# A weight gradient's block products: Strassen's seven for eight in ten of 32 pairs of slices

## The chip, the cores and the metric

The kernel runs on one core of a Trainium2 chip. The metric is the device time of one execution in microseconds; the kernel before takes 176.07 us (median of 3 runs, 175.95 to 176.48). The profiled execution spans 174.3 us from its first to its last instruction.

## The reference

```python
batch, m, k, n = 16, 512, 1024, 768      # float32 inputs, drawn from a normal distribution

def reference(input, grad_output):
    grad_weight = np.einsum('bmk,bmn->kn', input, grad_output)
    return grad_weight.astype(np.float32)
```

With batch and m joined, this is one matrix product: OUT (1024 x 768) = X^T G, with X of 8192 x 1024 and G of 8192 x 768, summed over 8192 rows. Both kernels cut the rows into 64 slices of 128 rows. A slice of X is 128 partitions by 1024 columns, a slice of G is 128 by 768. Both are turned to bf16 on their way into SBUF (the first ones by VectorE and ScalarE), are multiplied on TensorE and summed in fp32.

## The kernel before

TensorE multiplies one slice in twelve matmuls that are all 512 columns wide. The output's first 512 columns are computed as they stand: eight tiles of 128 rows of OUT (parts A and B, four tiles each), with X as the stationary operand. The last 256 columns (part N) are computed transposed: G's columns are stationary, X moves, and the result is turned back by VectorE in 32 x 32 blocks before it is stored.

```python
P = 128
NA = 512
WARMUP = [512] * 10 + [128] * 2
XBUFS = 42
...
    nc.sync.dma_start(out=gf[:, 0:NA], in_=G[0:P, 0:NA])
    nc.scalar.dma_start(out=xf[0], in_=X[0:P, :])
    nc.sync.dma_start(out=gf[:, NA:N], in_=G[0:P, NA:N])
    nc.scalar.dma_start(out=xf[1], in_=X[P : 2 * P, :])
...
    for s in range(1, S):
        gt = xg.tile([P, N], bf16, name="gt")
        nc.gpsimd.dma_start(out=gt, in_=G[s * P : (s + 1) * P, :])
        ...
        if s > 1:
            xs[s] = xg.tile([P, K], bf16, name="xt")
            nc.gpsimd.dma_start(out=xs[s], in_=X[s * P : (s + 1) * P, :])
...
    def add_out(dst, src):
        nc.vector.tensor_add(out=dst, in0=src, in1=dst)
...
    def wide_mm(bank, k, s, start, stop, c0=0, c1=NA):                       # parts A and B
        nc.tensor.matmul(
            bank, xs[s][:, k * P : (k + 1) * P], gwide[s][:, c0:c1], start=start, stop=stop
        )

    def narrow_mm(bank, t, h, s, start, stop):                               # part N
        nc.tensor.matmul(
            bank,
            gnarrow[s].rearrange("p (r t) -> p t r", t=NT)[:, t],
            xs[s][:, h * NA : (h + 1) * NA],
            start=start, stop=stop,
        )
```

A part accumulates slices in its four PSUM banks (each 128 x 512 fp32; there are eight banks) until it is closed, marked `!` in the order. Then each bank is copied (the first time) or added to a sum in SBUF, and the bank can be opened by another part:

```python
ORDER = (
    "A1! B1 N1 B2! N2 A2 N3! A3 B3 A4! B5 N5 B6! N7 A6 N8! A9! B10 N9 B12! N12! A12! "
    "B15 AB17! n17! AB26! n26! AB41! n41! AB47 A50! B50! N64!"
).split()
...
        dst = part.dst(*group)
        if part.first:
            copy_out(dst, bank, i)
            if s == 0 and i == 0:
                round_by("DVE", g0, gf, NA, N)
        else:
            add_out(dst, bank)
...
    for k in range(KS):
        slices = range(parts["A" if k < KS // 2 else "B"].done, S)
        pieces = [(0, NA)] if k < KS - 1 else [(0, 256), (256, 384), (384, NA)]
        for c0, c1 in pieces:
            ...
            for s in slices:
                wide_mm(bank, k, s, s == slices[0], s == slices[-1], c0, c1)
            add_out(acc[:, k, c0:c1], bank)
            ...
                nc.sync.dma_start(out=OUT[:, k, c : c + W], in_=acc[:, k, c : c + W])
```

"B15", for example, means: bring part B up to slice 15; "A50!" means: up to slice 50, and close. After the order the last 14 slices of A and B are done bank by bank, and every finished row tile is stored.

Of the kernel before, what the change touches and what calls it, by code (L numbers as in the profile page):

```python
# [6 lines left out]


P = 128
NA = 512  # L10
SQ = 32

ORDER = (
    "A1! B1 N1 B2! N2 A2 N3! A3 B3 A4! B5 N5 B6! N7 A6 N8! A9! B10 N9 B12! N12! A12! "
    "B15 AB17! n17! AB26! n26! AB41! n41! AB47 A50! B50! N64!"
).split()  # L20

WARMUP = [512] * 10 + [128] * 2
XBUFS = 42


@with_exitstack
def kernel(
# [6 lines left out]
    nc = tc.nc  # L34
    bf16 = mybir.dt.bfloat16
    f32 = mybir.dt.float32

    B, M, K = input.shape
    _, _, N = grad_output.shape
    S = B * M // P  # L40
    KS = K // P
    NB = N - NA
    NT = NB // P
    KH = K // NA

    X = input.rearrange("b m k -> (b m) k")
    G = grad_output.rearrange("b m n -> (b m) n")
    OUT = out.rearrange("(ks p) n -> p ks n", p=P)

    head = ctx.enter_context(tc.tile_pool(name="head", bufs=1))  # L50
    xg = ctx.enter_context(tc.tile_pool(name="xg", bufs=XBUFS))
    accp = ctx.enter_context(tc.tile_pool(name="accp", bufs=1))
    psum = ctx.enter_context(tc.tile_pool(name="psum", bufs=1, space=bass.MemoryType.PSUM))

    acc = accp.tile([P, KS, NA], f32, name="acc")
    acct = accp.tile([P, NT, K], f32, name="acct")


    turned = accp.tile([P, K // SQ, SQ, NT], f32, name="turned")


    xs = [None] * S
    gwide = [None] * S
    gnarrow = [None] * S

    E = mybir.EngineType
    ctx.enter_context(tc.manual_schedule(engines={E.PE, E.DVE, E.Activation}))


    xf = [head.tile([P, K], f32, name=f"xf{s}") for s in range(2)]  # L70
    gf = head.tile([P, N], f32, name="gf")
    nc.sync.dma_start(out=gf[:, 0:NA], in_=G[0:P, 0:NA])
    nc.scalar.dma_start(out=xf[0], in_=X[0:P, :])
    nc.sync.dma_start(out=gf[:, NA:N], in_=G[0:P, NA:N])
    nc.scalar.dma_start(out=xf[1], in_=X[P : 2 * P, :])


    ones = nc.const_aps.tensor(1.0, (P, P), bf16)
    wps = psum.tile([P, NA], f32, name="bank7")
    for i, cols in enumerate(WARMUP):  # L80
        nc.tensor.matmul(  # L81
            wps[:, 0:cols],
            ones,
            nc.const_aps.tensor(1.0, (P, cols), bf16),
            start=True,
            stop=True,
        )


    for s in range(1, S):  # L90
        gt = xg.tile([P, N], bf16, name="gt")
        nc.gpsimd.dma_start(out=gt, in_=G[s * P : (s + 1) * P, :])  # L92
        gwide[s] = gt[:, 0:NA]
        gnarrow[s] = gt[:, NA:N]
        if s > 1:
            xs[s] = xg.tile([P, K], bf16, name="xt")
            nc.gpsimd.dma_start(out=xs[s], in_=X[s * P : (s + 1) * P, :])  # L97

    for s in range(2):
        xs[s] = head.tile([P, K], bf16, name=f"x{s}")  # L100
    g0 = head.tile([P, N], bf16, name="g0")
    gwide[0] = g0[:, 0:NA]
    gnarrow[0] = g0[:, NA:N]

    def round_by(engine, dst, src, c0, c1):
        copy = nc.vector.tensor_copy if engine == "DVE" else nc.scalar.copy
        copy(out=dst[:, c0:c1], in_=src[:, c0:c1])  # L107

    round_by("DVE", g0, gf, 0, 256)
    round_by("ACT", g0, gf, 256, NA)  # L110
    round_by("DVE", xs[0], xf[0], 0, P)
    round_by("ACT", xs[0], xf[0], 2 * P, 4 * P)
    round_by("DVE", xs[0], xf[0], P, 2 * P)
    round_by("DVE", xs[0], xf[0], 4 * P, 6 * P)
    round_by("ACT", xs[0], xf[0], 6 * P, 8 * P)

    def add_out(dst, src):
        nc.vector.tensor_add(out=dst, in0=src, in1=dst)  # L118

    def copy_out(dst, src, i):  # L120
        if i % 2 == 0:
            nc.vector.tensor_copy(out=dst, in_=src)  # L122
        else:
            nc.scalar.copy(out=dst, in_=src)  # L124

    def wide_mm(bank, k, s, start, stop, c0=0, c1=NA):
        nc.tensor.matmul(  # L127
            bank, xs[s][:, k * P : (k + 1) * P], gwide[s][:, c0:c1], start=start, stop=stop
        )

    def narrow_mm(bank, t, h, s, start, stop):


        nc.tensor.matmul(  # L134
            bank,
            gnarrow[s].rearrange("p (r t) -> p t r", t=NT)[:, t],
            xs[s][:, h * NA : (h + 1) * NA],
            start=start,
            stop=stop,
        )  # L140

    class Part:
        def __init__(self, matmul, groups, dst):
            self.matmul = matmul
            self.groups = groups
            self.dst = dst
            self.done = 0
            self.first = True
            self.banks = {}

    wide_dst = lambda k: acc[:, k, :]
    narrow_dst = lambda t, h: acct[:, t, h * NA : (h + 1) * NA]
    parts = {
        "A": Part(wide_mm, [(k,) for k in range(KS // 2)], wide_dst),
        "B": Part(wide_mm, [(k,) for k in range(KS // 2, KS)], wide_dst),
        "N": Part(narrow_mm, [(t, h) for h in range(KH) for t in range(NT)], narrow_dst),
    }
    free = [f"bank{i}" for i in range(8)]

    def open_bank(part, i):  # L160
        name = free.pop(0)
        part.banks[i] = (name, psum.tile([P, NA], f32, name=name))

    def add_slice(part, i, s, first, last):
        group = part.groups[i]
        name, bank = part.banks[i]
        part.matmul(bank, *group, s, first, last)
        if not last:
            return
        dst = part.dst(*group)  # L170
        if part.first:
            copy_out(dst, bank, i)
            if s == 0 and i == 0:
                round_by("DVE", g0, gf, NA, N)
        else:
            add_out(dst, bank)
        if part is parts["N"] and s == S - 1:
            t, h = group
            hb = NA // SQ
            nc.vector.transpose(  # L180
                out=turned[:, h * hb : (h + 1) * hb, :, t],
                in_=dst.rearrange("p (b r) -> p b r", r=SQ),
            )
        free.append(name)
        del part.banks[i]
        if not part.banks:
            part.first = False

    def slice_by_slice(names, upto, close):
        while any(parts[n].done < upto for n in names):  # L190
            for n in names:
                part = parts[n]
                s = part.done
                if s == upto:
                    continue
                part.done += 1
                first = not part.banks
                for i in range(len(part.groups)):
                    if first:
                        open_bank(part, i)  # L200
                for i in range(len(part.groups)):
                    add_slice(part, i, s, first, close and s == upto - 1)

    def bank_by_bank(part, upto):
        first = part.done
        part.done = upto
        for i in range(len(part.groups)):
            open_bank(part, i)
            for s in range(first, upto):
                add_slice(part, i, s, s == first, s == upto - 1)  # L210

    for i, step in enumerate(ORDER):
        if i == 2:

            round_by("DVE", xs[1], xf[1], 4 * P, 6 * P)
            round_by("ACT", xs[1], xf[1], 6 * P, 8 * P)
            round_by("DVE", xs[1], xf[1], 0, 2 * P)
            round_by("ACT", xs[1], xf[1], 2 * P, 4 * P)
        close = step.endswith("!")
        names = step.rstrip("!").rstrip("0123456789")  # L220
        upto = int(step.rstrip("!").lstrip("ABNn"))
        if names.islower():
            bank_by_bank(parts[names.upper()], upto)
        else:
            slice_by_slice(names, upto, close)

    rows_of = out.rearrange("(b r) n -> r b n", r=SQ)
    for a in range(P // SQ):
        c = NA + a * NT * SQ
        nc.scalar.dma_start(  # L230
            out=rows_of[:, :, c : c + NT * SQ],
            in_=turned[a * SQ : (a + 1) * SQ].rearrange("p b r t -> p b (r t)"),
        )


    for k in range(KS):
        slices = range(parts["A" if k < KS // 2 else "B"].done, S)
        pieces = [(0, NA)] if k < KS - 1 else [(0, 256), (256, 384), (384, NA)]
        for c0, c1 in pieces:
            name = free.pop(0)  # L240
            bank = psum.tile([P, NA], f32, name=name)[:, 0 : c1 - c0]
            for s in slices:
                wide_mm(bank, k, s, s == slices[0], s == slices[-1], c0, c1)
            add_out(acc[:, k, c0:c1], bank)
            free.append(name)
            W = NB if k < 6 else c1 - c0
            for c in range(c0, c1, W):
                nc.sync.dma_start(out=OUT[:, k, c : c + W], in_=acc[:, k, c : c + W])


# [28 lines left out]
```

## Time and profile before

| | before |
|---|---|
| device time | 176.07 us (175.95 to 176.48) |
| span of the profiled execution | 174.3 us, 2013 instructions |
| matmuls of 512 columns, parts A and B (L127) | 489 recorded, modelled length 379 ns each |
| matmuls of 512 columns, part N (L134) | 250 recorded, 379 ns each |
| weight loads, 128 x 128 bf16 | 98 ns each |
| VectorE adding a 512-column bank to its sum | 683 ns each |
| bytes read from HBM, written to it | 58.72 MB, 3.15 MB |
| granted TensorE clock | 1.000 |

Engines are named PE (TensorE, with its weight loads as PEld), DVE (VectorE), ACT (ScalarE), POOL (GpSimd) and SP (SyncE, here an issuer of stores). L127 means line 127 of the kernel. A matmul's recorded length overlaps the next one's, so the busy time of PE says little of its pace; a few matmuls are missing from the records. In a line of groups or of the timeline, "128x512 f32<-128x512 f32" is the shape and type of output and input; what stands in brackets at its end is how long the engine stood idle just before, and what released it.

### The profile page before, as it was taken

Reading aid. Unit: us, or ns where it says so; the run is one execution under the profiler, and the core shown is the slowest. Engines: PE = TensorE matmul, PEld = TensorE weight load, DVE = VectorE, ACT = ScalarE, POOL = GpSimd, SP = SyncE. Lnnn points to the kernel's source line nnn. Section 1 sums busy time; section 2 is a strip of 40 time slices with the busy share of each in tenths; the row PEclk is TensorE's granted clock in tenths of the full one; section 3 lists DMA queues with packets and bytes.
Section 4 is the critical chain, followed back from the end, with each engine's and each line's share of the span. In section 5 each row is a group of like instructions: output and inputs, shape, how many; then the busy total and the mean of one; then the engine's idle time right before and its main releaser. Section 6 shows DMA issues by size and latency. Waiting matters only on the chain.

```text
span 174.3 us, 2013 instructions
## 1 busy us (share of the span) xinstructions
PE 169.9 (97%) x793; PEld 78.4 (45%) x808; DVE 61.3 (35%) x103; ACT 6.2 (4%) x12; POOL 66.7 (38%) x129
## 2 busy tenths in 40 slices
PE   8999999999999999999999999999999999999993
PEld 3444444444444444444444444444444444444463
DVE  0655582883940039300000662200560003931122
ACT  2640000000000000000000000000000000000000
POOL 7444434444444444444444444444274200000000
PEclk9999999999999999999999999999999999999999
DMA  5999999999999999999999999999999990085623
GB/s 192 276 208 209 207 209 208 208 208 209 207 208 209 207 208 210 207 209 209 206 209 208 208 210 207 207 209 208 207 209 209 207 202 11 0 190 160 170 86 120
DMA packets 25048, 33.35 MB, mean 191 GB/s; under 512 B 6480, under 2 KB 16592, under 8 KB 25040
## 3 DMA queue, kind: packets, MB, share of 16 engines
q0 software_dynamic: 18000, 28.65, 89.9%
q10 hardware_dynamic: 4448, 2.10, 4.7%
q1 hardware_dynamic: 2592, 2.49, 4.2%
q8 instruction: 6, 0.10, 0.2%
q14 instruction: 2, 0.02, 0.0%
HBM read 58.72 MB, written 3.15 MB: 355 GB/s over the span
## 4 chain that ended last, share of the span: by engine, by line
PE 97%; issue 0%; DVE 0%
PE bank L127 63%; PE bank L134 32%; PE bank L81 3%; DVE acc L118 0%
## 5 line engine op out<-in xcount | busy, mean ns | idle before, releaser
L127 PE MATMUL bank<-gt,xt 128*128 128x512 bf16 (+2 forms) x515 | 108.3, 367 | 0.5
L127 PEld LDWEIGHTS <-xt 128*128 128x128 bf16 x524 | 50.2, 98 | 57.2
L118 DVE TENSOR_TENSOR acc<-bank,acc 128x512 f32<-128x512 f32 (+2 forms) x62 | 37.9, 667 | 73.4 <-PE bank L127 72.9
L134 PE MATMUL bank<-xt,gt 128*128 128x512 bf16 x242 | 54.8, 379 | 0.3
L97 POOL DMA_DIRECT2D xt<-in_input_dram x62 | 33.1, 533 | 38.7 <-DMA xt<-in_input_dram 36.5
L92 POOL DMA_DIRECT2D gt<-in_grad_output_dram x63 | 33.8, 536 | 31.2 <-DMA gt<-in_grad_output_dram 24.9
L134 PEld LDWEIGHTS <-gt 128*128 128x128 bf16 x252 | 24.6, 98 | 29.7
L118 DVE TENSOR_TENSOR acct<-bank,acct 128x512 f32<-128x512 f32 x24 | 15.7, 682 | 30.0 <-PE bank L134 29.9
L81 PE MATMUL bank<-const-bfloat16-1.0 128*128 128x512 bf16 (+1 forms) x12 | 4.6, 574 | 0.8 <-PEq L263 0.8
L81 PEld LDWEIGHTS <-const-bfloat16-1.0 128*128 128x128 bf16 x12 | 1.6, 140 | 3.5 <-issue 3.5
L122 DVE COPY acc<-bank 128x512 f32<-128x512 f32 x4 | 2.7, 687 | 1.0 <-PE bank L127 1.0
L180 DVE STREAM_TRANSPOSE turned<-acct 128x512 f32<-128x512 f32 x4 | 2.9, 715 | 0.1
L127 PEld LDWEIGHTS <-x 128*128 128x128 bf16 x16 | 1.6, 98 | 1.9 <-DVE x L107 0.2
L107 DVE CAST g<-gf 128x256 bf16<-128x256 f32 x2 | 0.6, 290 | 4.7 <-DMA gf<-in_grad_output_dram 4.7
L124 ACT COPY acc<-bank 128x512 f32<-128x512 f32 x4 | 2.1, 589 | 1.3 <-PE bank L127 1.3
L127 PE MATMUL bank<-gt,x 128*128 128x512 bf16 x8 | 2.1, 379 | 0.0
L127 PE MATMUL bank<-g,x 128*128 128x512 bf16 x8 | 2.0, 398 | 0.0
L122 DVE COPY acct<-bank 128x512 f32<-128x512 f32 x2 | 1.3, 686 | 1.3 <-PE bank L134 1.3
L107 ACT CAST x<-xf 128x256 bf16<-128x256 f32 x4 | 1.4, 409 | 0.0
L107 ACT ACT_TABLE_LOAD x1 | 1.3, 1283 | 1.7 <-PEq L263 1.7
L124 ACT COPY acct<-bank 128x512 f32<-128x512 f32 x2 | 1.1, 588 | 1.5 <-PE bank L134 1.5
L107 DVE CAST x<-xf 128x256 bf16<-128x256 f32 (+1 forms) x5 | 1.0, 260 | 0.0
(8 smaller groups left out, 3.3 us busy)
## 6 DMA issues: line engine op xcount, KB each, us to landing
xt<-in_input_dram POOLq DMA_DIRECT2D x62, 256.0 KB, 8.5
gt<-in_grad_output_dram POOLq DMA_DIRECT2D x63, 192.0 KB, 8.5
out_dram<-acc SPq DMA_DIRECT2D x13, 128.0 KB, 2.7
xf<-in_input_dram ACTq DMA_DIRECT2D x2, 512.0 KB, 5.1
out_dram<-turned ACTq DMA_DIRECT2D x4, 256.0 KB, 3.4
gf<-in_grad_output_dram SPq DMA_DIRECT2D x1, 256.0 KB, 3.9
out_dram<-acc SPq DMA_DIRECT2D x1, 256.0 KB, 2.0
gf<-in_grad_output_dram SPq DMA_DIRECT2D x1, 128.0 KB, 4.7
```

Of the source, the lines that this page charges most:

```text
L81: nc.tensor.matmul(wps[:, 0:cols], ones, nc.const_aps.tensor(1.0, (P, cols), bf16), start=True, stop=True,)
L92: nc.gpsimd.dma_start(out=gt, in_=G[s * P : (s + 1) * P, :])
L97: nc.gpsimd.dma_start(out=xs[s], in_=X[s * P : (s + 1) * P, :])
L107: copy(out=dst[:, c0:c1], in_=src[:, c0:c1])
L118: nc.vector.tensor_add(out=dst, in0=src, in1=dst)
L122: nc.vector.tensor_copy(out=dst, in_=src)
L124: nc.scalar.copy(out=dst, in_=src)
L127: nc.tensor.matmul(bank, xs[s][:, k * P : (k + 1) * P], gwide[s][:, c0:c1], start=start, stop=stop)
L134: nc.tensor.matmul(bank, gnarrow[s].rearrange("p (r t) -> p t r", t=NT)[:, t], xs[s][:, h * NA : (h + 1) * NA], start=start, stop=stop,)
L180: nc.vector.transpose(out=turned[:, h * hb : (h + 1) * hb, :, t], in_=dst.rearrange("p (b r) -> p b r", r=SQ),)
```

## The change

The 64 slices are taken as 32 pairs. In 22 pairs each slice is multiplied plainly, now in sixteen matmuls of 384 columns: four parts A, B, C, D for the four quarters of OUT (upper and lower 512 rows, left and right 384 columns), each with four row tiles. Nothing is computed transposed any more.

In ten pairs the two slices (0 and 1) with the halves of X's and G's columns (left L, right R) form a 2 x 2 block product, which Strassen's scheme does with seven block products in place of eight, so 28 matmuls in place of 32. As the code forms them:

- m = (X0L + X1R)^T (G0L + G1R), n = (X0R + X1R)^T G0L, o = X0L^T (G0R - G1R), p = X1R^T (G1L - G0L), q = (X0L + X1L)^T G1R
- (X1L - X1R)^T (G1L + G1R) goes straight into part A, (X0R - X0L)^T (G0L + G0R) straight into part D
- at the end A gets m + p - q, B gets o + q, C gets n + p, and D gets m - n + o.

VectorE builds the sums and differences of X and G in bf16 (six instructions a pair) and combines the five product sums in fp32 (24 instructions at the end). A planned order says which part takes which slices when, when its four banks are closed, and how many of VectorE's extra instructions are queued before each bank's copy ("6,0,0,0") or before a step ("12A35"). Two parts of four banks are open at most. The purpose is less work for TensorE, with VectorE's free time in exchange.

The diff, cut to its core:

```diff
-NA = 512
-SQ = 32
+LOADS = "sssssssssssssssPsPPPPPPPPPssssss"
 ORDER = (
-    "A1! B1 N1 B2! N2 A2 N3! A3 B3 A4! B5 N5 B6! N7 A6 N8! A9! B10 N9 B12! N12! A12! "
-    "B15 AB17! n17! AB26! n26! AB41! n41! AB47 A50! B50! N64!"
+    "A1 C1!0,0,0,0 D1 D2!0,0,0,0 A2 B1 B2!0,0,0,0 A3 C2 C3 A4!0,0,0,0 C4 B3 B5!0,0,0,0 C5 "
+    "D6!0,0,0,0 A7 C8 A8 C9!0,0,0,0 A9 D9 A10!0,0,0,0 D10 B8 B11 B12 D11 B13!0,0,0,0 D12 D13 "
+    "C10 D14 C11 C12 D15!0,0,0,0 C13 C14 A11 C15 A12 A13 A14 C16 C17 A15 C18 A16 A17 "
+    "C19!0,0,0,0 A18 A19 B14 B15 B16 B17 B18 B19 B20 A20 B21 A21 A22 B22 A23 A24!0,0,0,0 B23 "
+    "B24 D16 D17 D18 D19 D20 D21 D22 D23 D24 B25 D26 D27 D28 D29!0,0,0,0 B27 C20 C21 C22 C23 "
+    "C24 C25 B28 C26 B30 C27 C28 C30 B32!6,0,0,0 C32!0,0,0,0 A25 A26 A27 A28 A29 D30 D31 D32 "
+    "D33 A30 A32 12A35!0,0,0,1 m3!0,0,1,0 q2 D34 q3 4q4!2,0,0,0 D35 o1 D36!2,0,0,0 o3 p2 p3 "
+    "o4 p4 2o5 p5 6o6!1,0,0,0 p6 n1 n2 n4 5p7!0,0,0,0 n5 D37 D38 D39!4,0,0,0 n6 n7 A37 A38 "
+    "2n8!3,0,0,0 A39 A40 m4 m5 m7 m8 3A41 6m10!0,0,0,0 p10!0,0,0,0 A43 q5 q6 q8 q10!0,0,0,0 "
+    "o10!0,0,0,0 n10!0,0,0,0 A46 B36 B38 A48 B40 A52 B42 B44!16,0,0,0 A54!0,0,0,0 D46 D50 "
+    "D54!8,0,0,0 C44!0,0,0,0 "
 ).split()
-XBUFS = 42
+PAIRS_HELD = 14
+SUMS_HELD = 9
... (loads: one tile of X and one of G for each pair, 14 of each held)
+    def sum_g1(i):
+        nc.vector.tensor_add(out=ge[:, 0:2, :], in0=g[:, :, 0, :], in1=g[:, :, 1, :])
+    def sum_g2(i):
+        nc.vector.tensor_add(out=extra[i][1][:, 2, :], in0=gp[:, 0, 0:NH], in1=gp[:, 1, NH:N])
+    def sum_g3(i):
+        nc.vector.tensor_sub(out=g[:, 1:3, :], in0=g[:, 1:3, :], in1=g[:, 3::-3, :])
+    def sum_x1(i):
+        nc.vector.tensor_add(out=xe[:, 0:2, :].rearrange("p a k -> p (a k)"), in0=xp[:, 0, :], in1=xp[:, 1, :])
+    def sum_x2(i):
+        nc.vector.tensor_add(out=extra[i][0][:, 2, :], in0=xp[:, 0, 0:KH], in1=xp[:, 1, KH:K])
+    def sum_x3(i):
+        nc.vector.tensor_sub(out=x[:, 1:3, :], in0=x[:, 1:3, :], in1=x[:, 0::3, :])
... (combining, each for q in 0..3)
+    def share(row, slots, q):
+        dst = acc[:, row + q, :].rearrange("p (h n) -> p h n", h=2)
+        nc.vector.tensor_add(out=dst, in0=dst, in1=macc[:, slots, q, :])
+    def top3(q):
+        c = acc[:, q, 0:NH]
+        nc.vector.tensor_sub(out=c, in0=c, in1=macc[:, 4, q, :])
... (top1, top2, low1, low2 call share; low3 is like top3)
+        def shut(q):
+            fill(ahead[q])                       # the extra VectorE instructions queued here
+            if carried or (fresh[p] and q in COPIED):      # COPIED = (1, 3), carried is never set
+                nc.scalar.copy(out=dst, in_=bank)
+            elif fresh[p]:
+                nc.vector.tensor_copy(out=dst, in_=bank)
+            else:
+                nc.vector.tensor_add(out=dst, in0=bank, in1=dst)
+            if final and p in "ABCD":
+                nc.sync.dma_start(out=OUT[:, row, c0 : c0 + NH], in_=dst)
... (a step with one slice: its four matmuls, then the four banks' copies; with several: bank by bank)
... (the very last bank is done as 256 and 128 columns)
+        if n == 2:                               # ahead of the third step, D1
+            round_by("DVE", g0, gf, NH, N)
+            round_by("DVE", x1, xf[1], 4 * P, 6 * P)
+            ...
```

In the order a number counts what a part takes: plain slices and pairs for A and D, plain slices for B and C, pairs for m to q.

## The prediction

> **What bounds the kernel now.** I read the busy times and the chain of waits first, then the groups with shapes kept apart, then the waits, and last three stretches of the timeline: the end, the beginning and the load queue. Busy times (engine, busy us, share, instructions) and the chain that ended last:
>
> ```profile
> PE 169.9 (97%) x793; PEld 78.4 (45%) x808; DVE 61.3 (35%) x103; ACT 6.2 (4%) x12; POOL 66.7 (38%) x129
> ...
> PE 97%; issue 0%; DVE 0%
> PE bank L127 63%; PE bank L134 32%; PE bank L81 3%; DVE acc L118 0%
> ```
>
> The matmuls alone carry the chain: nothing but the warm-up (L81), the two kinds of matmul and one last addition is on it. A matmul's end is modelled, so I take its pace from the VectorE additions that wait for each finished bank. The end of the timeline (start us, us, engine, line, operation):
>
> ```profile
> 159.34 0.69 DVE L118 TENSOR_TENSOR acc<-bank,acc 128x512 f32<-128x512 f32 x1 [2.33 <-PE bank L127]
> 162.37 0.69 DVE L118 TENSOR_TENSOR acc<-bank,acc 128x512 f32<-128x512 f32 x1 [2.33 <-PE bank L127]
> 165.39 0.69 DVE L118 TENSOR_TENSOR acc<-bank,acc 128x512 f32<-128x512 f32 x1 [2.33 <-PE bank L127]
> 168.41 0.69 DVE L118 TENSOR_TENSOR acc<-bank,acc 128x512 f32<-128x512 f32 x1 [2.33 <-PE bank L127]
> 169.94 0.42 DVE L118 TENSOR_TENSOR acc<-bank,acc 128x256 f32<-128x256 f32 x1 [0.84 <-PE bank L127]
> 170.72 0.29 DVE L118 TENSOR_TENSOR acc<-bank,acc 128x128 f32<-128x128 f32 x1 [0.36 <-PE bank L127]
> 171.50 0.29 DVE L118 TENSOR_TENSOR acc<-bank,acc 128x128 f32<-128x128 f32 x1 [0.49 <-PE bank L127]
> ```
>
> Each bank here takes slices 50 to 63, 14 matmuls. So 512 columns take (168.41 - 159.34) / 42 = 215.9 ns, 256 columns 1.53 / 14 = 109.3, 128 columns 0.78 / 14 = 55.7: a straight line, 0.417 ns a column and 2.3 ns a matmul. At 384 columns that is 162.5 ns. As a test, 754 matmuls of 215.9 and 14 split ones (109.3 + 2 x 55.7) make 165.9 us; from the first real matmul at 5.42 that ends at 171.3, which is where they end. TensorE stands still nowhere.
>
> The first DVE and ACT work, and the load queue (POOL), give the supply:
>
> ```profile
> 4.71 0.29 DVE L107 CAST g<-gf 128x256 bf16<-128x256 f32 x1 [4.71 <-DMA gf<-in_grad_output_dram]
> 5.04 0.56 DVE L107 CAST x<-xf 128x128 bf16<-128x128 f32 x3
> 5.89 0.69 DVE L122 COPY acc<-bank 128x512 f32<-128x512 f32 x1 [0.28 <-PE bank L127]
> 6.50 0.28 DVE L107 CAST g<-gf 128x256 bf16<-128x256 f32 x1
> ...
> 13.66 2.48 DVE L118 TENSOR_TENSOR acc<-bank,acc 128x512 f32<-128x512 f32 x4 [1.30 <-PE bank L127]
> ```
>
> ```profile
> 9.98 0.53 POOL L97 DMA_DIRECT2D xt<-in_input_dram  x1 [0.71 <-DMA xt<-in_input_dram]
> ...
> 12.19 0.53 POOL L97 DMA_DIRECT2D xt<-in_input_dram  x1 [0.72 <-DMA xt<-in_input_dram]
> ...
> 14.39 0.53 POOL L97 DMA_DIRECT2D xt<-in_input_dram  x1 [0.70 <-DMA xt<-in_input_dram]
> ```
>
> Three things are to be seen. The second half of the first gradient slice is rounded right behind one copy-out. Four additions of 512 take 2.48 us, so they start (2.48 - 0.69) / 3 = 0.60 us apart: 533 ns of elements (1.04 ns each) and about 66 ns. And the queue goes on each time an older input slice has landed, one per 2.2 us, so slice s has landed at about 5.55 + 2.2 s, the last at 144 us. The kernel before spends 12 x 215.9 = 2.59 us on a slice; loads run ahead of it.
>
> [...]
>
> **The change part by part.** *TensorE.* 44 slices stay plain, 16 matmuls each (8 row tiles, 2 halves): 704. Ten pairs take 7 products of 4: 280. Together 984, by 162.5 ns: 159.9 us against 165.9. That is 6.0 us less, all on the chain. Columns fall by 4% (984 x 384 against 768 x 512), but there are 216 more matmuls at 2.3 ns, 0.5 us, already in these sums. Weight loads (98 ns) fit beneath 162 ns; they did beneath shorter matmuls at the end too.
>
> *Front.* The second half of g0 is now rounded only after C1 has been closed. A1 and C1 are 8 matmuls, so D1 could start at 5.42 + 1.30 = 6.72. C1's first bank is ready for VectorE 0.41 us after its issue at 6.07 (0.325 for the matmul by its modelled length, 0.09 as seen before). VectorE copies two banks at a pitch of 66 + 400 = 466 ns, from 6.48 to 7.41, then rounds 384 columns: from 224 and 285 ns for 128 and 256 columns about 350 ns. D1 begins at about 7.83: a loss of 1.1 us that wasn't there. Afterwards each slice takes 16 x 162.5 = 2.60 us, again more than 2.2, so the supply holds; the tightest is slice 4, landed at 14.35 and wanted at about 15.1.
>
> *VectorE, sums.* A pair needs six additions over 768, 384, 768, 1024, 512 and 1024 elements, 4480. At double speed (0.52 ns) this is 2.33 us and 6 x 0.066 = 2.7 us, for ten pairs 27 us. *Closings.* 32 times four banks; nine closings are first ones, where ScalarE takes two of the four, so VectorE has 110 of 466 ns: 51 us. *Combining.* 16 fp32 additions of 768 elements (0.87 us) and 8 of 384 (0.47): 18 us. Together 96 us of VectorE's queue in about 161: 60%, none of it on the chain by itself, but unevenly spread.
>
> *The crowded stretch.* From 84 us (C32 copied out) to 124 (m10 copied out) VectorE does nine pairs' sums, 24.6 us, and nine closings, 36 banks less the ten that ScalarE takes: 26 x 0.466 = 12.1. That is 36.7 in 40 us. Adding up the order step by step with these durations, each sum is done before its matmul, at times with only half a microsecond to spare. I find no wait there.
>
> *The combining.* 16 of 24 combining additions stand in VectorE's queue before B's closing, from 135 us on, when n10 is copied out. Two that update the same rows follow one another with the full latency (about 0.96 + 0.05 instead of 0.87), so the 16 take about 13 us and end at about 148.3; B's bank is wanted back for D at 148.7. At most 0.2 us is lost. The other eight stand before D's closing and run beneath D and C.
>
> *End.* As before: last additions split into 256 and 128 columns, then a 64 KB store. Gone are the strided gradient weights, four 32 x 32 transposes and their stores, all off the chain.
>
> *Buffers.* Pair u takes the place of pair u - 14. Pair 15 is wanted at about 66 us and pair 1 is free by 20; pair 28 is wanted at 123 and pair 14 is free at 80. No load should wait.
>
> Sum: 176.07 - 6.0 + 1.1 + 0.2 + 0.2 for small waits on banks = 171.6 us.
>
> **Rivals.** (1) *VectorE becomes the bound between 84 and 124 us.* If bf16 additions run at single speed, a pair costs 2.33 us more, nine pairs 21 us, with 3.3 us of slack: about 18 us more, 189 us. Less extreme: 54 sums and 26 copies that each cost 80 ns more than I took add 6.4 us to 36.7, 3 to 5 us of waits: 175 us. For it: the stretch is 92% full by my count, and pitches of two-input SBUF additions are not in the trace. [...] (2) *Bank turns.* Eight banks now serve two open parts of four, and a closing of one slice needs four copies of 0.47 us before another part may open. If handshakes cost 0.1 us more than I took, some ten turns lose 0.05 to 0.4 us each: 1 to 2 us, 173 us. For it: there is little spare bank space; against it: nearly always another open part stands between closing and opening. (3) *The front costs nothing*, because ScalarE and VectorE share the copies more luckily or the half slice is rounded before C1's banks are ready: 170.4 us. Against it: queue order. (4) *The supply stays the limit.* Loads end at 144 us whatever TensorE does, but before, 27 us of matmuls remained after that and now about 22 remain, so they are hidden.
>
> **Range and chances.** The count of matmuls and their pace are firm: 170.1 is the least. To the 1.1 of the front I add 0.4, and the right tail is rival 1 and 2. I take 171.6, with 170.1 to 174.5 for 8 in 10. Two per cent is 172.55: 0.95 us of further waits use it up. Faster by over 2%: 0.70; within 2%: 0.24; slower by over 2%: 0.06.
>
> **What would show it.** Right: matmuls of 384 columns 162 to 163 ns apart; one pause of about 1 us before D1 near 7 us; TensorE's idle time elsewhere under 1 us; bf16 additions of 1024 elements near 0.69 us; the last real matmul issued near 166.5; POOL waiting only for landed transfers. Wrong: waits of matmuls for DVE sums or banks from 84 to 124 us (rival 1), many small waits of 0.1 to 0.4 us from 9 us on (rival 2), a matmul pace over 163 ns, or POOL waiting for TensorE.

## The result, and the profile after

| | before | after |
|---|---|---|
| device time, median | 176.16 us (175.95 to 176.48, 4 runs) | 171.95 us (171.77 to 172.04, 4 runs) |
| ratio | | 0.976 (95% interval 0.975 to 0.978) |
| span of the profiled execution | 174.3 us | 170.2 us |

The change makes the kernel 2.4% faster; 171.6 us was predicted. Busy times and the chain of waits of the changed kernel:

```profile
PE 165.5 (97%) x1008; PEld 98.8 (58%) x1008; DVE 102.0 (60%) x202; ACT 10.8 (6%) x24; POOL 66.6 (39%) x129
...
PE 97%; DVE 1%; issue 0%
PE bank L267 93%; PE bank L83 3%; PE bank L317 1%; DVE acc L283 1%; DVE acc L325 0%; DVE gp L194 0%
```

Matmuls carry the chain as before, with one new guest at the front: DVE. The same chain in order of time (start us, us, what) shows where it comes in:

```profile
0.78 4.64 PE bank L83 x12
5.41 1.46 PE bank L267 x5
6.87 0.02 issue
6.89 1.02 DVE acc L283 x2
7.92 0.28 DVE gp L194
8.19 0.04 issue
8.24 156.97 PE bank L267 x964
```

Two copies of C1's banks, then the rounding of g0's second half (gp, L194), then D1 at 8.24 us; after that 964 matmuls without a stop, 156.97 / 964 = 162.8 ns apart. VectorE's new work in the costliest groups (engine, operation, shape, count, busy us, mean ns, idle before):

```profile
L153 DVE TENSOR_TENSOR acc<-acc,macc 128x768 f32<-128x768 f32 x16 | 15.3, 954 | 0.2
...
L144 DVE TENSOR_TENSOR xp<-xp 128x1024 bf16<-128x1024 bf16 x10 | 6.9, 690 | 0.0
L135 DVE TENSOR_TENSOR xe<-xp 128x1024 bf16<-128x1024 bf16 x10 | 6.9, 689 | 0.0
...
L139 DVE TENSOR_TENSOR xe<-xp 128x512 bf16<-128x512 bf16 x10 | 4.2, 422 | 0.0
...
L164 DVE TENSOR_TENSOR acc<-acc,macc 128x384 f32<-128x384 f32 x4 | 2.2, 558 | 0.1
```

From 512 to 1024 bf16 elements the time grows from 422 to 690 ns, 0.52 ns an element; from 384 to 768 fp32 elements it grows from 558 to 954 ns, 1.03 ns an element. So a two-input addition takes half as long an element in bf16 as in fp32. The prediction's 0.52 ns was an assumption, half of the 1.04 ns seen for fp32: no bf16 addition runs in the kernel before. And how full VectorE is, by stretches (us, PE busy, weight loads, DVE, ACT, POOL, clock, DMA share, GB/s):

```profile
84.00:100.00 16.00, 16.00 (x100) 9.64 (x99) 14.73 (x33) 1.82 (x4) 7.79 (x15) 1.00 1.14 208
100.00:124.00 24.00, 24.00 (x150) 14.45 (x148) 22.72 (x50) 2.58 (x6) 11.60 (x22) 1.00 1.14 209
...
135.00:150.00 15.00, 15.00 (x93) 8.96 (x92) 14.65 (x21) 0.00 (x0) 1.14 (x3) 1.00 0.69 127
```

In the crowded stretch DVE is busy 37.45 of 40 us while PE never pauses. Only the sum fits the forecast so far; which of its terms hold is what the experiments are for.

### The profile page after: what moved, and what is told of

It is laid out like the page before. It is cut to its first block, busy times and chain, and to the rows that moved or that the text cites. A ratio compares the mean times of both kernels' runs of the same rounds, so it can differ in the third digit from the quotient of the medians.

```text
span 170.2 us, 2538 instructions
## 1 busy us (share of the span) xinstructions
PE 165.5 (97%) x1008; PEld 98.8 (58%) x1008; DVE 102.0 (60%) x202; ACT 10.8 (6%) x24; POOL 66.6 (39%) x129
## 4 chain that ended last, share of the span: by engine, by line
PE 97%; DVE 1%; issue 0%
PE bank L267 93%; PE bank L83 3%; PE bank L317 1%; DVE acc L283 1%; DVE acc L325 0%; DVE gp L194 0%
## 5 line engine op out<-in xcount | busy, mean ns | idle before, releaser
L267 PE MATMUL bank<-gp,xp 128*128 128x384 bf16 x772 | 130.2, 327 | 0.9 <-DVE gp L194 0.9
L267 PEld LDWEIGHTS <-xp 128*128 128x128 bf16 x852 | 83.5, 98 | 56.6 <-issue 1.9
L285 DVE TENSOR_TENSOR acc<-bank,acc 128x384 f32<-128x384 f32 x71 | 35.0, 551 | 48.1 <-PE bank L267 47.8
L103 POOL DMA_DIRECT2D xp<-in_input_dram x62 | 33.0, 533 | 36.9 <-DMA xp<-in_input_dram 32.1
L101 POOL DMA_DIRECT2D gp<-in_grad_output_dram x63 | 33.7, 535 | 33.5 <-DMA gp<-in_grad_output_dram 23.4
L267 PE MATMUL bank<-ge,xp 128*128 128x384 bf16 x80 | 16.9, 326 | 0.0
L267 PEld LDWEIGHTS <-xe 128*128 128x128 bf16 x120 | 11.7, 98 | 7.8
L153 DVE TENSOR_TENSOR acc<-acc,macc 128x768 f32<-128x768 f32 x16 | 15.3, 954 | 0.2
L267 PE MATMUL bank<-gp,xe 128*128 128x384 bf16 x80 | 14.3, 326 | 0.0
L285 DVE TENSOR_TENSOR macc<-bank,macc 128x384 f32<-128x384 f32 x20 | 9.7, 550 | 3.9 <-PE bank L267 3.8
```

The source lines that it names most:

```text
L101: nc.gpsimd.dma_start(out=gp[:, h, :], in_=G[s * P : (s + 1) * P, :])
L103: nc.gpsimd.dma_start(out=xp[:, h, :], in_=X[s * P : (s + 1) * P, :])
L153: nc.vector.tensor_add(out=dst, in0=dst, in1=macc[:, slots, q, :])
L267: nc.tensor.matmul(bank, stat, mov, start=opening and j == 0 and not carried, stop=close and j == len(items_now) - 1, skip_group_check=car ...
L285: nc.vector.tensor_add(out=dst, in0=bank, in1=dst)
```

## The experiments

All times are medians, set against a kernel before that ran on the same chip in the same group (175.96 to 176.06 us).

**Rounding g0's second half early.** Theory: the pause before D1 is queue order and costs 1.1 us. Rivals: data, or bank turns.

```diff
     round_by("ACT", x0, xf[0], 6 * P, 8 * P)
+    round_by("DVE", g0, gf, NH, N)          # ahead of the copies that close C1
 ...
-            round_by("DVE", g0, gf, NH, N)  # at the third step
```

> The rounding of g0's second half is queued right behind x0's roundings on VectorE, ahead of the copies that close C1; nothing else changes. Theory (queue order at the front costs 1.1 us): D1's first matmul no longer waits for the rounding; it then waits only for C1's first bank to be copied, about 0.4 us, and loads of slices 3 and 4 may take back 0.1 to 0.3 us. So 171.9 becomes 171.2 to 171.5, and the pause before D1 shrinks from 1.1 to about 0.4 us. Rival (the pause only hides a wait for data: slice 1's gradient lands at 7.8 us and later slices follow every 2.2 us): the time stays at 171.9 and the pause moves to matmuls that wait for loads. Rival (bank turn alone sets the pause): same time, D1 waits as long for bank copies.

Measured: 172.16 us (171.91 to 172.51), ratio 0.978 (0.976 to 0.979): nothing gained. TensorE in the timeline of this run, two pieces from its beginning (in brackets the idle time before, and what ended it):

```profile
6.99 3.55 PE L269 MATMUL bank<-gp,xp 128*128 128x384 bf16 x20 [0.33 <-DVE acc L285]
10.71 75.57 PE L269 MATMUL bank<-gp,xp 128*128 128x384 bf16 x464 [0.17 <-DMA xp<-in_input_dram]
```

and one from near its end:

```profile
143.45 3.73 PE L269 MATMUL bank<-gp,xp 128*128 128x384 bf16 x22 [0.63 <-DMA gp<-in_grad_output_dram]
```

D1 does begin at 6.99 us, after a short wait for a bank. But then a slice of X is waited for at 10.7, and at 143.45 a gradient: 0.63 us. The pause went to the loads, as the first rival said, and the wait at 143 us stands where neither the prediction nor this expectation had placed one. The first wait is for slice 2. In the chain of waits of this run the load of its X is issued at 2.93 us, behind three loads of G, and lands 7.73 us later:

```profile
2.93 7.73 DMA xp<-in_input_dram
```

**Each x0 + x1 made twice.** Theory: VectorE is nearly the bound from 84 to 124 us.

```diff
             f(i)
+            if f is sum_x1:
+                f(i)
```

> The bf16 addition over 1024 elements that makes x0 + x1 is issued twice in each of the ten pairs (the second writes the same values again): 0.60 us more of VectorE's queue a pair, 5.4 us in nine pairs between 84 and 124 us. Theory (VectorE is nearly the bound there: 36.7 of 40 us counted, 37.4 recorded busy): matmuls begin to wait for sums and banks, about 3 us in all, 174.5 to 176. Rival (VectorE has room to spare because sums can slide): within 0.5 us of 171.9.

Measured: 175.73 us (175.19 to 176.44), ratio 0.997 (0.994 to 0.999), 3.8 us more than the changed kernel. TensorE's pieces with a pause in this run, and the same stretches:

```profile
92.19 0.34 PE L269 MATMUL bank<-ge,xp 128*128 128x384 bf16 x1 [0.44 <-DVE xp L144]
...
100.22 0.95 PE L269 MATMUL bank<-gp,xp 128*128 128x384 bf16 x4 [0.38 <-DVE macc L285]
...
109.67 2.90 PE L269 MATMUL bank<-gp,xe 128*128 128x384 bf16 x16 [0.31 <-DVE macc L285]
...
126.67 1.31 PE L269 MATMUL bank<-ge,xe 128*128 128x384 bf16 x7 [1.06 <-DVE xe L139]
```

```profile
84.00:100.00 16.00, 15.39 (x94) 8.96 (x93) 15.46 (x33) 1.82 (x4) 7.94 (x15) 1.00 1.14 208
100.00:124.00 24.00, 23.48 (x137) 13.26 (x137) 23.82 (x50) 2.58 (x6) 11.46 (x22) 1.00 1.14 208
```

Matmuls wait for sums (xp, xe) and for banks that VectorE hasn't emptied (macc), and VectorE is busy 39.3 of 40 us. The added instructions are an estimated 5.4 us (0.60 us of queue in each of nine pairs) and cost some 3.8 us. This profiled execution also waited 0.9 us for a load at 22.7 us, before any of the doubled sums of this stretch; the fastest of the four (175.19) is only 3.2 us over the changed kernel. So the room was about 1.6 to 2.2 us, as an estimate.

**Plain matmuls of 384 columns, no Strassen.** Theory: the seven products bring 40 matmuls and nothing else.

```diff
-LOADS = "sssssssssssssssPsPPPPPPPPPssssss"
+LOADS = "ssssssssssssssssssssssssssssssss"
 (the order as it was up to C32, then A and D to 46, B and C to 58, and the rest part by part)
```

> No pair is combined: all 32 pairs are multiplied plainly in 384-column matmuls, 1024 in all, in parts A to D with the same beginning of the order, and an order of the same manner after that; no bf16 sums, no combining. Theory (the seven products bring 40 matmuls of 162.8 ns, and nothing else of size): 6.5 us more than the changed kernel, 178.4 us, 2.3 us more than the kernel before, of which about 0.8 us is the 256 more matmuls' fixed part, 1.5 us the front. Rival (Strassen's gain is partly given back by waits in the crowded stretch): plain 384 is less than 6 us slower, 177 to 178.

Measured: 179.08 us (179.06 to 179.47), ratio 1.017 (1.016 to 1.019). From D1 at 7.56 us, 1016 matmuls of 162.8 ns would end at 173.0; in the chain of waits the last ends at 173.7, so this order of mine has 0.7 us of waits of its own. To set the two kernels side by side, take the second profile of the changed kernel (below), which begins at the same pace, with D1 at 7.54: its matmuls end at 167.11, 6.6 us earlier, and 0.56 us of waiting for a load are in that. 6.6 - 0.7 + 0.56 makes 6.4, against 40 x 162.8 ns = 6.5: TensorE is spared all of Strassen's 40 matmuls, and the load takes 0.56 us of this gain back. (The medians are 7.1 us apart, because the plain kernel also takes 0.6 us longer from its last matmul to its end, 3.6 against 3.0 us.) Against the kernel before, the plain kernel of 384 columns loses 3.0 us; 0.7 us of this are the waits of this one order, so the price of cutting the matmuls to 384 columns is not measured clean of it.

**No combining.** The 24 additions of the product sums to the output are left out, so these products are missing from the output.

```diff
-            f(i)
+            if f not in (top1, top2, top3, low1, low2, low3):
+                f(i)
```

> The 24 fp32 combining additions are left out, so the five product sums are not added to the output. Theory (they run beneath matmuls; B's bank comes back at most 0.2 us late): 171.7 to 171.95, no difference that can be measured. Rival (they delay the last closings and stores): 0.5 to 1.5 us faster.

Measured: 171.88 us (171.75 to 172.02), ratio 0.976 (0.975 to 0.977). The combining is hidden, although in the changed kernel VectorE is busy 14.65 of 15 us while the larger part of it runs.

**The changed kernel once more.**

> The changed kernel as it is, once more, as the yardstick of this group and for a second look at its beginning. In its first profile the first four real matmuls ran at half pace (0.32 us apart, 0.6 us lost); in three kernels with the same beginning they did not. If that is chance of the single execution, this profile shows D1 at about 7.6 us or 8.2 us, and the time stays 171.8 to 172.0.

Measured: 171.92 us (171.86 to 172.16), ratio 0.977 (0.975 to 0.978). TensorE's three starts after an idle time in this profile:

```profile
5.17 1.47 PE L267 MATMUL bank<-gp,xp 128*128 128x384 bf16 x8 [0.58 <-DVE xp L194]
7.54 78.86 PE L267 MATMUL bank<-gp,xp 128*128 128x384 bf16 x484 [0.89 <-DVE gp L194]
143.34 6.17 PE L267 MATMUL bank<-gp,xp 128*128 128x384 bf16 x37 [0.56 <-DMA gp<-in_grad_output_dram]
```

This is the most telling profile of the study. D1 begins 0.70 us earlier than in the first profile of the very same kernel (7.54 against 8.24), and the end is the same: the last matmul group ends at 167.11 here and at 167.20 there. The 0.7 us is given back at 143.34 in a wait for a gradient. So in the first profile two bounds met: TensorE's own work and the landing of one slice. The profile without the combining shows the same as the second one: D1 at 7.59 us, and a wait of 0.45 us for a gradient at 143.24. The weight loads of the first profile show why it began late:

```profile
5.18 0.18 PEld L267 LDWEIGHTS <-xp 128*128 128x128 bf16 x2
5.53 0.15 PEld L267 LDWEIGHTS <-xp 128*128 128x128 bf16 x1 [0.17 <-ACT xp L194]
5.85 0.15 PEld L267 LDWEIGHTS <-xp 128*128 128x128 bf16 x1 [0.17 <-issue]
6.17 0.15 PEld L267 LDWEIGHTS <-xp 128*128 128x128 bf16 x1 [0.17 <-issue]
6.49 0.63 PEld L267 LDWEIGHTS <-xp 128*128 128x128 bf16 x4 [0.17 <-issue]
```

From 5.2 to 6.5 us they come 0.32 us apart, twice the later pitch: four matmuls at half pace, 4 x (0.32 - 0.163) = 0.63 us.

Which load is waited for at 143 us? The load queue of the changed kernel near its end:

```profile
127.37 0.54 POOL L101 DMA_DIRECT2D gp<-in_grad_output_dram  x1 [3.31 <-issue]
127.90 0.54 POOL L103 DMA_DIRECT2D xp<-in_input_dram  x1
128.42 0.55 POOL L101 DMA_DIRECT2D gp<-in_grad_output_dram  x1
128.94 1.74 POOL L103 DMA_DIRECT2D xp<-in_input_dram  x3
131.38 0.53 POOL L103 DMA_DIRECT2D xp<-in_input_dram  x1 [0.71 <-PE bank L267]
132.35 0.53 POOL L103 DMA_DIRECT2D xp<-in_input_dram  x1 [0.43 <-DMA xp<-in_input_dram]
133.54 0.53 POOL L101 DMA_DIRECT2D gp<-in_grad_output_dram  x1 [0.67 <-PE bank L267]
134.55 0.53 POOL L101 DMA_DIRECT2D gp<-in_grad_output_dram  x1 [0.48 <-DMA xp<-in_input_dram]
135.77 0.53 POOL L101 DMA_DIRECT2D gp<-in_grad_output_dram  x1 [0.69 <-DMA gp<-in_grad_output_dram]
136.75 0.53 POOL L101 DMA_DIRECT2D gp<-in_grad_output_dram  x1 [0.45 <-DMA xp<-in_input_dram]
```

The program writes G and X by turns, but the queue of GpSimd was put together otherwise: five loads of X in a row, then the last four of G, slices 60 to 63. In the second profile's chain the load that ends the wait was issued at 134.47, the second of the four (slice 61), and landed 8.84 us later. Step A52 wants this slice as its fourth matmul, and 145 matmuls, 23.8 us, stand behind it (that one counted, and the split bank as twelve). The queue also stood idle for 3.3 us ahead of these loads, for no reason that the profile shows ("issue"). The kernel before has such a pause of 3.25 us at the same place, and the transfers went on meanwhile at 208 GB/s; whether slice 61 would land earlier without it is not tested.

**Loads in the program's order.**

```diff
-    ctx.enter_context(tc.manual_schedule(engines={E.PE, E.DVE, E.Activation}))
+    ctx.enter_context(tc.manual_schedule(engines={E.PE, E.DVE, E.Activation, E.Pool}))
```

> Only the order of the load queue is changed: the program's own order, G and X by turns to the end. In the changed kernel the queue's last nine entries are five loads of X and then four of G, so that the gradients of slices 60 to 63 land last, at about 140.5 to 144.5 us. Theory (the end is set by the gradient of slices 60 and 61, landed at 143.4, and by the 23.8 us of matmuls that stand behind it): slice 61 lands about 140, no matmul waits for a load near 143, and the time falls by what the wait was, 0.4 to 0.7 us, to 171.2 to 171.6. Rival (matmuls alone set the end): 171.9.

Measured: 171.91 us (171.40, 171.82, 172.01, 172.05), ratio 0.976 (0.974 to 0.978). The profile is that of the 171.40, and its chain of waits has no wait for a load any more:

```profile
7.36 0.28 DVE gp L194
7.64 0.04 issue
7.68 156.97 PE bank L267 x964
164.65 1.99 PE bank L317 x24
```

D1 at 7.68 us, and the end of the matmuls at 166.64 in place of 167.11. Slice 61's gradient is now issued at 131.17 us in place of 134.47. So the wait at 143 us did come from the order of the loads. But the median has not moved, and so the expected time was missed in three executions of four. The next two experiments take up whether half-pace beginnings explain this.

**Both: early rounding and loads in order.**

> The load queue in the program's order and the early rounding of g0's second half together. Theory (front: what the early rounding wins is lost again to slices 2 to 4, which land no earlier): at most 0.3 us better than loads in order alone, 171.0 to 171.5. Rival (the early rounding was only spoilt by the wait at 143 us): 0.8 to 1.1 us better than loads in order alone, 170.4 to 170.7.

Measured: 171.29 us (171.09 to 171.52), ratio 0.973 (0.972 to 0.974). This beats both kernels: 0.6 us better than the changed one. The time lies in the range of the theory; the gain over loads in order alone, 0.6 us by the medians, lies between the theory's 0.3 and the rival's 0.8. The chain of its profile:

```profile
1.17 5.45 DMA gf<-in_grad_output_dram
6.62 0.02 issue
6.64 0.36 DVE gp L194
7.00 0.48 DVE acc L285
7.47 0.04 issue
7.52 156.96 PE bank L269 x964
```

What D1 waits for now is the landing of g0's second half (gf, at 6.62 us), its rounding, and the copy of C1's first bank. No matmul waits for a load after that, not even for slice 2 at 10.7 us. The one word that orders the end of the load queue also orders its beginning: the load of slice 2's X is issued at 2.41 us, in third place, where it was issued at 2.93 with early rounding alone. In the profile of this kernel's second round:

```profile
2.41 0.55 POOL L103 DMA_DIRECT2D xp<-in_input_dram  x1
```

So this edit takes away both of the waits that early rounding ran into; which share of the gain belongs to which of them is not separated.

**Loads in order, and both, once more.**

> The kernel with loads in the program's order, once more, because its four times fell apart (171.4, then 171.8 to 172.05). Theory (with the loads in order nothing at 143 us levels out any more whether TensorE's first four real matmuls ran at half pace or not, 0.6 us): times spread from 171.3 to 172.1, and a profile with a half-pace beginning (D1 at 8.2 us) belongs to about 172.0, one with a full-pace beginning (D1 at 7.6 us) to about 171.4. Rival (the order of loads does nothing, and the single 171.4 was chance): 171.8 to 172.1 whatever the beginning.

> The kernel with early rounding and loads in order, once more, to set it against the one without early rounding in the same group. Theory: 171.0 to 171.5, better than loads in order alone by 0.3 us where that one begins at full pace and by 0.7 us where it begins at half pace. Rival: no difference from it.

Measured: loads in order alone 171.72 us (171.22, 171.62, 171.82, 172.17), ratio 0.975 (0.973 to 0.977); both 171.29 us (171.04 to 171.52, and one at 172.01), ratio 0.974 (0.972 to 0.976). The profile of the first is that of its 171.82, with a half-pace beginning and D1 at 8.25 us; the one of the group ahead of it, 171.40, began at full pace. With early rounding the profile of 171.04 began at full pace with D1 at 7.30. So the eight times of "loads in order" spread from 171.2 to 172.2, where the nine of the changed kernel lie within 171.8 to 172.2, and the two profiled executions fall on the expected sides. That the other six are explained by the beginning is likely, but not shown: only profiled executions show it. Of the nine times of both edits together, eight are 171.52 or less; this gain is clear of the noise.

**Product n without six of its ten pairs.** 24 matmuls are left out, so the output lacks these products; all sums and closings stay.

```diff
         def mm(q, j):
+            if p == "n" and upto in (2, 4, 5, 6, 7):
+                return
```

> As the changed kernel, but product n leaves out six of its ten pairs (24 matmuls, 3.9 us of TensorE, between 107 and 114 us); all sums, closings and loads stay. Theory (in this stretch TensorE has no lead over VectorE's sums, and later none over the last loads): matmuls wait instead, first for sums of the seventh to ninth pair, 3 us in all, then at 143 us for the load, and the time stays within 0.3 us of 171.9. Rival (TensorE sets the time throughout, as the chain of waits reads): 3.9 us less, 168.0.

Measured: 170.52 us (170.27 to 170.78), ratio 0.969 (0.967 to 0.970): 1.4 us less, for 3.9 us of matmuls less. Neither expectation was met. TensorE's pieces with a pause:

```profile
109.97 2.25 PE L269 MATMUL bank<-ge,xp 128*128 128x384 bf16 x12 [1.20 <-DVE macc L285]
112.71 2.53 PE L269 MATMUL bank<-ge,xp 128*128 128x384 bf16 x12 [0.49 <-DVE acc L287]
```

From D1 at 8.30 us, 952 matmuls of 162.8 ns would end at 163.3; they end at 165.99. So 2.7 of the 3.9 us turned into waits for VectorE, about what was expected of the sums; from 106.6 to 112.7 us the chain of waits of this run goes through VectorE's sums and bank copies alone. The second part of the expectation, a wait at 143 us, did not come, because leaving out the matmuls also changed the load queue: near its end X and G came mostly by turns. That part stays untested in this run.

## Why the prediction was right, and where it was not

- *Number and pace of the matmuls* (6.0 us). Right. They run 162.8 ns apart where 162.5 was taken, which makes 0.3 us over all of them; the plain kernel confirms Strassen's share (6.4 us for 40 matmuls).
- *Front* (a loss of 1.1 us). The mechanism is shown by the chain: the rounding stands behind two copies, and D1 waits 1.07 us for it at full pace (from 6.47, eight matmuls after 5.17, to 7.54). But removing the pause brought nothing by itself, since slice 2 landed no earlier (10.66 us), and the wait at 143 us levelled the rest. With both obstacles gone, early rounding is worth 0.4 us between the two full-pace profiles (matmuls end at 166.64 and 166.27); the rest of the 1.07 us goes to the landing of g0's second half and to the bank copy. "The supply holds" was right only because the pause hid the wait for slice 2.
- *VectorE's sums* and *the crowded stretch*. Right: the bf16 additions take the assumed 0.52 ns an element, 36.7 us are counted and 37.45 recorded in 40, no matmul waits. The doubled addition and the cut product show from both sides that this stretch has only about 2 us to spare and that TensorE can't go faster there. Rival 1 was a near miss; its milder form is what the doubled addition produced.
- *The combining*. Right: B's bank was not waited for, and without the additions the time is the same. The second of two additions of 768 to the same rows starts 0.99 us after the first (1.01 was taken), and the 16 end at 148.8 us (148.3 was taken).
- *Rival 2, bank turns*. Fell: no matmul of the changed kernel waits for a bank after D1. One of the signs of being wrong did appear, POOL waiting for TensorE: seven waits, 4.7 us together, two of them in the lines above. They do not speak for a lack of buffers. The kernel before has four of the same kind, 5.2 us with its pause of 3.25, and the place that slice 60's load takes at 133.54 us (pair 16's) had seen its last matmul before m3, about 40 us earlier.
- *Buffers* ("No load should wait") and *rival 4* ("they are hidden"). This is the step that failed. I argued that 22 us of matmuls remain after the last load, so loads can't matter. What counts is not how much work remains but whether it could be done earlier: behind the gradient of slice 61 stand 23.8 us of matmuls in a fixed order. It landed at 143.3 us, when TensorE, at full pace, had been out of work for 0.56 us. I took the program's order of loads for the queue's order; with it, my own rule would have landed slice 61 at 5.55 + 2.2 x 61 = 139.8 us.
- *The sum.* From 176.16: -6.0 for the matmuls, +1.07 for the front, +0.56 for the load, +0.3 for the pace make 172.1; 171.95 was measured. (In an execution that begins at half pace, the loss there stands in the load's place.) The 0.4 us that I had set aside for waits on banks, B's among them, did not come, and 0.9 us for a load and the pace, which I had not foreseen, came instead. That the total is still within 0.4 us is partly luck.

## What to carry to other kernels

When a kernel is bound by one engine, find out by how much: count for each stretch how far the loads and the helper engines are ahead. Here TensorE reads as the bound in 97% of the chain, yet VectorE has about 2 us to spare in 40 and one load none at all, so a microsecond saved in front of such a place is simply waited out there. Look at the queue's real order of loads, not at the program's: the last gradients stood behind five loads of the other input, and one word in the scheduling call put this right. It brought something only together with the early rounding (171.29 us): alone, neither edit moved the median by more than the noise.

## What the runs showed of the hardware

- The beginning differs from execution to execution of one kernel. Four real matmuls at half pace (0.32 us for 384 columns) are seen in some profiles and one or none in others, while the granted clock is recorded as 1.00 over the first 8 us. In the first profile of the changed kernel the warm-up's weight loads come 0.43 us apart, twice the 215.9 ns of 512 columns, the last of them starts at 5.00 us, and the half pace ends at about 6.5 us. With early rounding alone the warm-up's last weight load has ended by 4.35 us (0.83 us before the first real one at 5.18); if it took 0.10 us, as in the last profile of this kernel with loads in order, it started 0.75 us earlier than 5.00, so by my estimate the half pace ended there at about 5.00 - 2 x 0.75 = 3.5 us. What sets this moment no run shows.
- VectorE's two-input bf16 additions and GpSimd's issuing of loads ran side by side, and neither took visibly longer for it. An issue took 533 to 535 ns, as before (533 to 536), the ten additions that make x0 + x1 took 684 to 696 ns each, and 208 GB/s flowed in the crowded stretch.
- Every matmul has a weight load, recorded at 98 ns. Matmuls nevertheless followed one another 162.8 ns apart, and 55.7 ns apart in the last 128-column pieces of the kernel before.
